# Depthwise convolution in eight phases: two channel tiles summed on VectorE, the other taps in half pairs, the last exchange on another queue

## The chip, the cores and the metric

The program runs on one core of one Trainium2 chip. The metric is the device time of one execution in microseconds (us). Before the change it is 1882.76 us, the median of three runs (1879.57 to 1883.23). The core has five engines that run side by side, each in its own order: PE (TensorE, with PEld, its weight load), DVE (VectorE), ACT (ScalarE), POOL (GpSimd) and SP (SyncE, which here only issues transfers). 0.2% of the time is 3.8 us.

## What is computed

Two model blocks are computed for 512 tokens of width 1024. The change touches one layer of the second block, a convolution module; everything else stands.

```
def conformer_conv(x, w_pw1, b_pw1, w_dw, b_dw, ln_g, ln_b, w_pw2, b_pw2):
    a = jax.nn.glu(x @ w_pw1 + b_pw1, axis=-1)
    y = lax.conv_general_dilated(
        a, w_dw[:, None, :].astype(a.dtype), window_strides=(1,),
        padding=((CONV_WIDTH - 1, 0),),
        dimension_numbers=('NWC', 'WIO', 'NWC'),
        feature_group_count=D_MODEL) + b_dw
    y = jax.nn.silu(layernorm(y, ln_g, ln_b))
    return y @ w_pw2 + b_pw2
```

`x` is the RMS-normed stream, 512 tokens by 1024 channels. The middle step is causal and depthwise: each channel has 31 taps (`CONV_WIDTH`), and each output token is the sum of 31 earlier gated values of the same channel, each times its tap. The layer norm then takes mean and variance over all 1024 channels of a token, so no token can be normalised before all channels are summed.

## The kernel before

Tensors stand with channels on the 128 partitions, so 1024 channels are 8 tiles (`t` = 0 to 7) of 128 x 512. A dense product is done in three fp32r matmuls for each weight block (high x high, high x low, low x high; lines 395 to 397). Its weights come in units of 128 x 1024. For each unit SP loads `raw` (line 338, two buffers), ACT rounds it into `wH` (line 373) and DVE subtracts to get `wL` (line 374).

`ph_con` computes the convolution module. For each tile `t` PE runs a **dense block**, the 48 matmuls of units 2t and 2t+1, which give the two halves of the gated unit. After the next dense block is written out, `open_gates(t)` puts on DVE: two scalings out of PSUM (`cg`, `ca`), a memset, and the gated product `glu` (line 1476); on ACT the sigmoid between them; then two weight splits (`wH`, `wL`) for the dense block after next; and, by `to_phases`, an **exchange** on SP: the tile is written to DRAM (`ph`*t*`x`, line 1425) and read back in eight pieces (`xp`, line 1428), so that the partitions hold 8 phases of the time axis x 16 channels. In this layout the 31 taps of 16 channels are 5 matrices of 128 x 128, and PE does the depthwise sum (`taps`, line 1438). Tiles are taken two by two: a pair is 80 matrix products, which the hardware runs as 160 matmuls of 64 columns each. The matrices come from DRAM, packed by the host in blocks (`mat`) of 16, 1 MB each, five for a pair, twenty in all. POOL issues them (line 1411) in the order of use, into the eight buffers that the activations `x` (four of them) also use.

DVE then adds the bias out of PSUM (`take`, line 1448) into `Y` and takes the layer norm's statistics (line 1453). When the last pair is through, a short serial stretch makes mean and scale (lines 1521 to 1537), and the output product follows.

Each engine runs its instructions in the order in which the code is written. This is the order that the change touches:

```
                    open_gates(t - 1)
                    if t in (4, 6):
                        pair(t // 2 - 2)
                    if t in (5, 7):
                        taken(t // 2 - 2)
                open_gates(last)
...
                pair(2)
                W = [self.unit(ahead=0) for _ in range(4)]
                taps(3, halves[0])
                taken(2)
```

So PE runs pair 0 after dense block 4, pair 1 after dense block 6, pair 2 after dense block 7, and pair 3 last; the exchange of tile 7 is issued by SP after `open_gates(7)`.

Of the kernel before, what the change touches and what calls it, by code (L numbers as in the profile page):

```python
# [10 lines left out]
F32 = mybir.dt.float32  # L11
# [42 lines left out]

RP, GC, NQ = 8, 16, 64

NMAT = 5
# [172 lines left out]
def matrix_order():  # L230

    return [(2 * i + j, g, m) for i in range(NT // 2) for g in range(P // GC) for m in range(NMAT) for j in range(2)]

# [37 lines left out]
class Builder:  # L271
# [1116 lines left out]
    def ph_con(self, ph):  # L1388
        nc, tc = self.nc, self.tc
        x = self.x  # L1390
        with tc.tile_pool(name="pc", bufs=1) as pool:
# [9 lines left out]
            nc.sync.dma_start(out=both, in_=self.kst_d[:, KC["both"][0]:KC["both"][0] + P])  # L1401
            gates, glus, xs, banks, mats = {}, {}, {}, {}, []
            place = {key: n for n, key in enumerate(matrix_order())}
# [15 lines left out]
            def padded(name):  # L1419
                return pool.tile([P, W_], F32, tag="glu", name=self.nm(name), bufs=8)  # L1420


            def to_phases(t):
                d = self.dp.tile([P, W_], F32, name=f"ph{t}x")
                nc.sync.dma_start(out=d, in_=glus.pop(t))
                xp = xs[t] = padded("xp").rearrange("p (g q) -> p g q", g=P // GC)
                for s in range(RP):
                    nc.sync.dma_start(out=xp[GC * s:GC * s + GC],
                                      in_=bass.AP(d.tensor, d.offset + s * q_, [[W_, GC], [GC * W_, P // GC], [1, q_]]))
# [21 lines left out]
            def statistics(i, b):  # L1451
                for r in range(RP):
                    nc.vector.bn_stats(stat[:, r, 2 * i + b, :], Y[:, i, r, b * 64:b * 64 + 64])

            halves = [range(4), range(4, 8)]

            def pair(i):
                for gs in halves:
                    taps(i, gs)

            def taken(i):
                for b, gs in enumerate(halves):
                    take(i, gs)
                    statistics(i, b)

            def open_gates(u):
                pa, pg = gates.pop(u)
                a, g = self.tmp(name="ca"), self.tmp(name="cg")
                nc.vector.tensor_tensor(g, pg, rb, ALU.mult)
                nc.vector.tensor_tensor(a, pa, rb, ALU.mult)  # L1470
                nc.scalar.activation(g, g, AF.Sigmoid, bias=self.col("b_pw1", 8 + u))
                glu = glus[u] = padded("glu")
                view = lambda v: v.rearrange("p (q r) -> p r q", r=RP)
                o = glu.rearrange("p (r q) -> p r q", r=RP)
                nc.vector.memset(o[:, :, :NMAT - 1], 0.0)
                nc.vector.scalar_tensor_tensor(o[:, :, NMAT - 1:], view(a), self.col("b_pw1", u), view(g),
                                               ALU.add, ALU.mult)
                to_phases(u)
                for _ in range(2):
                    if self.u_split <= self.u_used + 2:  # L1480
                        self.split()

            last = NT - 1
            with tc.manual_schedule():
# [5 lines left out]
                for t in range(1, NT):  # L1490
# [6 lines left out]
                    gates[t] = pa, pg  # L1497
                    open_gates(t - 1)
                    if t in (4, 6):
                        pair(t // 2 - 2)  # L1500
                    if t in (5, 7):
                        taken(t // 2 - 2)
                open_gates(last)

                nc.scalar.activation(self.small([P, 1]), self.ones[:, 0:1], AF.Silu)
                pair(2)
                W = [self.unit(ahead=0) for _ in range(4)]
                taps(3, halves[0])
                taken(2)

# [292 lines left out]
```

## Time and profile before

| what | us |
|---|---|
| median of three runs | 1882.76 |
| the profiled execution | 1881.89 |
| its span, first to last instruction | 1880.1 |
| PE busy (9386 matmuls) | 1839.6 (98%) |
| DVE busy | 941.0 (50%) |
| ACT busy | 696.0 (37%) |
| POOL busy | 242.9 (13%) |

The span is the stretch that the trace covers; the profiled execution's own time is 1.8 us more. PE is busy nearly all the time, so a change elsewhere moves the time only where PE stands still or is given less to do. Two of the 40 slices of the page (47 us each) show PE below 9 tenths. One of them, from 893 to 940 us, holds the end of the convolution module. PEclk is the clock that the throttle granted to PE; it has two levels, 2.4 GHz (shown as 1.00) and 1.2 GHz (0.50). The convolution module runs from 766.9 to about 984 us of the span.

### The profile page before, as it was taken

To read this page: it belongs to the slowest core of one execution; us is meant where nothing else is said; L and a number is where in the kernel's file an instruction comes from. 1 tells how busy PE (TensorE), PEld (TensorE's weight loads), DVE (VectorE), ACT (ScalarE), POOL (GpSimd) and SP (SyncE) were. 2 spreads that over 40 slices of the span, in tenths; PEclk is the share of its full clock that TensorE was granted. 3 is DMA by queue.
4 is the path that set the end of the run, shared out by engine and by line. 5 is a ranking of instruction groups with operands and counts; after the bars stand their busy time and mean duration, and the time that the engine had idled before them with its cause. 6 is when DMAs were issued, how large, how long until landed. Compare 5 with 4: busy or idle time off the path is not lost.

```text
span 1880.1 us, 23726 instructions
## 1 busy us (share of the span) xinstructions
PE 1839.6 (98%) x9386; PEld 1508.0 (80%) x9386; DVE 941.0 (50%) x1667; ACT 696.0 (37%) x1145; POOL 242.9 (13%) x243
## 2 busy tenths in 40 slices
PE   9999999999999999999799999999999999999997
PEld 6877778888888888878578888888877888888886
DVE  6567755655343444444455434335677543343444
ACT  5546644444232324212243222123566432232232
POOL 0111011020000001101021101011254211010110
PEclk9999999999999999999899999999999999999998
DMA  5223222132323323577223332654211223222321
GB/s 195 96 68 124 90 90 79 57 96 90 101 91 100 101 90 101 174 232 284 77 90 108 103 101 91 108 158 136 90 59 45 79 90 101 92 96 93 101 90 55
DMA packets 68112, 198.57 MB, mean 106 GB/s; under 512 B 15344, under 2 KB 23152, under 8 KB 65440
## 3 DMA queue, kind: packets, MB, share of 16 engines
q1 hardware_dynamic: 61744, 169.96, 28.2%
q0 software_dynamic: 3584, 24.12, 4.4%
q10 hardware_dynamic: 2672, 2.97, 0.5%
q8 instruction: 74, 1.21, 0.3%
q14 instruction: 38, 0.31, 0.0%
HBM read 189.55 MB, written 7.47 MB: 105 GB/s over the span
## 4 chain that ended last, share of the span: by engine, by line
PE 81%; issue 8%; DVE 4%; DMA 3%; ACT 2%; POOL 1%; SPq 0%; POOLq 0%; ACTq 0%; DVEq 0%
PE mm L395 25%; PE mm L396 25%; PE mm L397 24%; DVE wL L374 1%; DMA mat<-in_mat_dram 1%; DMA raw<-in_w_dram 1%; PE pc L1438 1%; ACT wH L373 1%; PE bo L1756 1%; DVE q L1664 1%; PE fs L879 1%; PE ft L894 1%; PE fo L907 1%; DMA ph7x<-glu 0%; PE bs L1713 0%
## 5 line engine op out<-in xcount | busy, mean ns | idle before, releaser
L373 ACT CAST wH<-raw 128x1024 fp32r<-128x1024 f32 (+1 forms) x304 | 315.9, 1041 | 910.1 <-PE mm L396 615.3
L395 PE MATMUL mm<-xH,wH 128*128 128x512 f32 x1232 | 482.4, 392 | 0.0
L396 PE MATMUL mm<-xL,wH 128*128 128x512 f32 x1232 | 480.5, 390 | 0.7 <-DVE xL L536 0.7
L397 PE MATMUL mm<-xH,wL 128*128 128x512 f32 x1232 | 480.4, 390 | 0.0
L374 DVE TENSOR_TENSOR wL<-raw,wH 128x1024 fp32r<-128x1024 f32 (+1 forms) x304 | 371.5, 1223 | 144.2 <-ACT wH L373 137.1
L395 PEld LDWEIGHTS mm<-xH,wH 128*128 128x128 f32 x1232 | 231.8, 188 | 49.7 <-issue 2.2
L396 PEld LDWEIGHTS mm<-xL,wH 128*128 128x128 f32 x1232 | 231.7, 188 | 48.6 <-DVE xL L536 1.1
L397 PEld LDWEIGHTS mm<-xH,wL 128*128 128x128 f32 x1232 | 231.5, 188 | 48.2
L395 PE MATMUL mm<-hidH,wH 128*128 128x512 f32 (+1 forms) x615 | 238.2, 387 | 0.0
L396 PE MATMUL mm<-hidL,wH 128*128 128x512 f32 (+1 forms) x615 | 238.1, 387 | 0.0
L397 PE MATMUL mm<-hidH,wL 128*128 128x512 f32 (+1 forms) x615 | 238.0, 387 | 0.0
L549 DVE TENSOR_TENSOR h<-mm,h 128x512 f32<-128x512 f32 x103 | 71.1, 691 | 262.4 <-PE mm L397 262.4
L498 POOL TENSOR_TENSOR ssq<-ssq,sq 128x512 f32<-128x512 f32 (+1 forms) x49 | 77.8, 1587 | 627.1 <-ACT sq L497 620.4
L1371 POOL TENSOR_TENSOR g<-g,rbc 128x512 f32<-128x512 f32 x44 | 75.0, 1705 | 538.7 <-ACT g L1370 538.7
L395 PEld LDWEIGHTS mm<-hidH,wH 128*128 128x128 f32 x615 | 115.5, 188 | 24.0 <-issue 0.6
L396 PEld LDWEIGHTS mm<-hidL,wH 128*128 128x128 f32 x615 | 115.6, 188 | 23.5
L397 PEld LDWEIGHTS mm<-hidH,wL 128*128 128x128 f32 x615 | 115.5, 188 | 23.3
L1372 DVE TENSOR_TENSOR g<-mm,g 128x512 f32<-128x512 f32 x44 | 30.1, 690 | 124.1 <-PE mm L397 119.5
L1369 DVE TENSOR_TENSOR g<-mm,rbc 128x512 f32<-128x512 f32 x44 | 30.2, 691 | 99.2 <-PE mm L397 97.6
L1338 DVE SCALAR_TENSOR_TENSOR u<-mm,rbc 128x512 f32<-128x512 f32 x32 | 22.0, 691 | 77.0 <-PE mm L397 75.8
L395 PE MATMUL mm<-wH,xH 128*128 128x512 f32 (+1 forms) x160 | 60.3, 377 | 0.0
L397 PE MATMUL mm<-wH,xL 128*128 128x512 f32 (+1 forms) x160 | 59.0, 369 | 0.0
(326 smaller groups left out, 2296.3 us busy)
## 6 DMA issues: line engine op xcount, KB each, us to landing
raw<-in_w_dram SPq DMA_DIRECT2D x272, 512.0 KB, 3.5
mat<-in_mat_dram POOLq DMA_DIRECT2D x20, 1024.0 KB, 9.7
raw<-in_w_dram SPq DMA_DIRECT2D x32, 448.0 KB, 3.2
rel<-rt POOLq DMA_DIRECT2D x1, 3072.0 KB, 36.3
h<-in_x_dram SPq DMA_DIRECT2D x8, 256.0 KB, 5.1
raw<-in_w_dram SPq DMA_DIRECT2D x8, 256.0 KB, 5.3
bias<-rel SPq DMA_DIRECT2D x1, 2048.0 KB, 8.8
mem<-in_mem_dram ACTq DMA_DIRECT2D x4, 256.0 KB, 4.4
```

What stands on the lines that cost most here:

```text
L373: self.nc.scalar.copy(H[:, :n], raw[:, :n])
L374: self.low = lambda: self.nc.vector.tensor_tensor(L[:, :n], raw[:, :n], H[:, :n].bitcast(F32), ALU.subtract)
L395: mm(out, lhsT=aH, rhs=bH, start=start, stop=False)
L396: mm(out, lhsT=aH, rhs=bL, start=False, stop=False)
L397: mm(out, lhsT=aL, rhs=bH, start=False, stop=stop)
L498: (eng or nc.gpsimd).tensor_tensor(self.ssq[:, :n], self.ssq[:, :n], q[:, :n], ALU.add)
L549: nc.vector.tensor_tensor(self.h[:, t, :], ps, self.h[:, t, :], ALU.add)
L879: nc.tensor.matmul(ps[j][:, :n], lhsT=q[rs, t, bs], rhs=k[rs, t, :n], start=x == 0, stop=False)
L1338: nc.vector.scalar_tensor_tensor(t, ps, 0.0, rb, ALU.max, ALU.mult)
L1369: nc.vector.tensor_tensor(g, pg, rb, ALU.mult)
L1371: nc.gpsimd.tensor_tensor(g, g, rb, ALU.mult)
L1372: nc.vector.tensor_tensor(g, pu, g, ALU.mult)
```

## The change

Tiles 0 and 1 (`DIRECT`) are not exchanged and need no matrices. DVE sums their 31 taps itself: 31 instructions for each tile, each over 128 x 512 values, alternating between two accumulators, and one addition of the two (`chains`). `fill` places these instructions among the others of `open_gates`, by the numbers in `CHAIN`. PE then turns the two sums into the layout of `Y` by products with the identity (`turned`), and DVE adds the bias (`taken_direct`).

Tiles 2 to 7 stay with the matrices, which are now 15 blocks. Their taps stand in half pairs of 40 matrix products: pair 1 after dense blocks 5 and 6, the first half of pair 2 after dense block 7, then the rest of pair 2 and pair 3. The exchange of tile 7 is issued by POOL, and ahead of it are the issues of the first eleven matrix blocks; the last four follow it. The shared buffers of `glu` and `xp` are six, not eight.

```diff
-    return [(2 * i + j, g, m) for i in range(NT // 2) for g in range(P // GC) for m in range(NMAT) for j in range(2)]
+    return [(2 * i + j, g, m) for i in range(1, NT // 2) for g in range(P // GC) for m in range(NMAT) for j in range(2)]
...
+DIRECT, CHAIN = [0, 1], (6, 8, 8, 8, 10, 14, 14, 8)
...
             def to_phases(t):
+
+                eng = nc.gpsimd if t == NT - 1 else nc.sync
                 d = self.dp.tile([P, W_], F32, name=f"ph{t}x")
-                nc.sync.dma_start(out=d, in_=glus.pop(t))
+                eng.dma_start(out=d, in_=glus.pop(t))
...
+            def chains():
+                for t in DIRECT:
+                    while t not in glus:
+                        yield
+                    acc = [pool.tile([P, S], F32, tag="cy", name=self.nm("cy"), bufs=3) for _ in range(2)]
+                    for k in range(TAPS):
+                        a, tap = acc[k % 2], glus[t][:, 2 + k:2 + k + S]
+                        if k < 2:
+                            nc.vector.tensor_scalar(a, tap, wd(t, k), None, ALU.mult)
+                        else:
+                            nc.vector.scalar_tensor_tensor(a, tap, wd(t, k), a, ALU.mult, ALU.add)
+                        yield
+                    nc.vector.tensor_tensor(acc[0], acc[0], acc[1], ALU.add)
+                    done[t] = acc[0]
+                    yield
...
+            def turned():
+
+                for b in range(2):
+                    ps = banks["direct", b] = self.bank("pc")
+                    for r in range(4):
+                        for j in range(2):
+                            nc.tensor.matmul(ps[j * NQ:j * NQ + NQ, r * P:(r + 1) * P],
+                                             lhsT=done[j][:, 4 * b + r::RP], rhs=self.ident, start=True, stop=True)
+
+            def taken_direct():
+                for b in range(2):
+                    nc.vector.tensor_tensor(Y[:, 0, 4 * b:4 * b + 4, :],
+                                            banks.pop(("direct", b)).rearrange("p (r c) -> p r c", r=4),
+                                            bdw[:, 0, :].unsqueeze(1).to_broadcast([P, 4, P]), ALU.add)
+                for b in range(2):
+                    statistics(0, b)
...
-            def open_gates(u):
+            def open_gates(u, steps):
...
                 nc.scalar.activation(g, g, AF.Sigmoid, bias=self.col("b_pw1", 8 + u))
+                fill(2)
                 glu = glus[u] = padded("glu")
...
                 for _ in range(2):
                     if self.u_split <= self.u_used + 2:
-                        self.split()
+                        self.split_high()
+                        fill(2)
+                        self.split_low()
+                fill(steps - 6)
...
-                    open_gates(t - 1)
-                    if t in (4, 6):
-                        pair(t // 2 - 2)
-                    if t in (5, 7):
-                        taken(t // 2 - 2)
-                open_gates(last)
+                    if t == last:
+                        load_matrices(11 - len(mats))
+                    open_gates(t - 1, CHAIN[t - 1])
+
+                    if t >= 5:
+                        i, b = (t - 3) // 2, (t - 5) % 2
+                        taps(i, halves[b])
+                    if t >= 6:
+                        taken((t - 4) // 2, (t - 6) % 2)
+                open_gates(last, CHAIN[last])
...
-                pair(2)
+                for _ in chain:
+                    pass
+                taps(2, halves[1])
+                taken(2, 0)
+                turned()
                 W = [self.unit(ahead=0) for _ in range(4)]
+                taken(2, 1)
                 taps(3, halves[0])
-                taken(2)
+                taken_direct()
```

How this moves the instructions shows on two engines. First DVE, between `glu` of tile 5 and the scalings of tile 6. Here `wL` is a weight split, `cg` and `ca` are the scalings out of the PSUM banks `mm`, `cY` is a `take`, `cst` the statistics, and `cy` the two accumulators of the new chain. Before:

```order
L1476 SCALAR_TENSOR_TENSOR glu_7026<-ca_7021,cst,cg_7022 128x8x64
L374 TENSOR_TENSOR wL_7041<-raw_6945,wH_7040 128x1024
L374 TENSOR_TENSOR wL_7047<-raw_6951,wH_7046 128x1024
L1469 TENSOR_TENSOR cg_7195<-mm_6972,rbc_6490 128x512
L1470 TENSOR_TENSOR ca_7194<-mm_6971,rbc_6490 128x512
```

After the change, DVE's rows from the second weight split of this block on:

```order
L1477 SCALAR_TENSOR_TENSOR cy_6877<-glu_6591,cst,cy_6877 128x512
L1477 SCALAR_TENSOR_TENSOR cy_6878<-glu_6591,cst,cy_6878 128x512
L1477 SCALAR_TENSOR_TENSOR cy_6877<-glu_6591,cst,cy_6877 128x512
L1477 SCALAR_TENSOR_TENSOR cy_6878<-glu_6591,cst,cy_6878 128x512
L1477 SCALAR_TENSOR_TENSOR cy_6877<-glu_6591,cst,cy_6877 128x512
L1477 SCALAR_TENSOR_TENSOR cy_6878<-glu_6591,cst,cy_6878 128x512
L1477 SCALAR_TENSOR_TENSOR cy_6877<-glu_6591,cst,cy_6877 128x512
L1477 SCALAR_TENSOR_TENSOR cy_6878<-glu_6591,cst,cy_6878 128x512
L1453 TENSOR_TENSOR cY<-pc_6883,cb 128x8x64
L1458 BN_STATS cst_6353<-cY 128x6 x8
L1509 TENSOR_TENSOR cg_7138<-mm_6927,rbc_6490 128x512
L1510 TENSOR_TENSOR ca_7137<-mm_6926,rbc_6490 128x512
```

Eight rows of the chain of tile 1 and one `take` with its statistics now stand ahead of the scalings of tile 6; six more rows of the chain stand earlier in the block.

Second POOL, its issues from the matrices of pair 2 on. `mat` is a matrix block, `ph7x` the copy of tile 7 in DRAM, `xp` its eight pieces (`x8`). Before, the last seven issues:

```order
L1411 DMA mat_7320<-in_mat_dram 128x2048
L1411 DMA mat_7338<-in_mat_dram 128x2048
L1411 DMA mat_7363<-in_mat_dram 128x2048
L1411 DMA mat_7381<-in_mat_dram 128x2048
L1411 DMA mat_7399<-in_mat_dram 128x2048
L1411 DMA mat_7436<-in_mat_dram 128x2048
L1411 DMA mat_7454<-in_mat_dram 128x2048
```

After, the last ten:

```order
L1414 DMA mat_7129<-in_mat_dram 128x2048
L1414 DMA mat_7131<-in_mat_dram 128x2048
L1414 DMA mat_7133<-in_mat_dram 128x2048
L1414 DMA mat_7135<-in_mat_dram 128x2048
L1430 DMA ph7x<-glu_7237 128x544
L1433 DMA xp_7242<-ph7x 16x8x68 x8
L1414 DMA mat_7353<-in_mat_dram 128x2048
L1414 DMA mat_7371<-in_mat_dram 128x2048
L1414 DMA mat_7408<-in_mat_dram 128x2048
L1414 DMA mat_7426<-in_mat_dram 128x2048
```

The exchange of tile 7 has come from SP's queue into POOL's, behind the first block of pair 3 and ahead of the four others.

## Rows read from the trace of the kernel before

**Rows 1.** The chain that ended last: start us, us, what.

```profile
882.97 1.17 DVE glu L1476
884.16 8.96 DMA ph7x<-glu
...
896.40 6.26 DMA xp<-ph7x
```

**Rows 2.** Timeline of PE: start us, us, line, out<-in, count [idle before <-releaser].

```profile
821.38 0.39 PE L395 MATMUL mm<-xH,wH 128*128 128x512 f32 x1
822.06 0.39 PE L395 MATMUL mm<-xH,wH 128*128 128x512 f32 x1
822.83 7.21 PE L1438 MATMUL pc<-mat,xp 128*64 128x128 f32 x128
833.73 3.68 PE L1438 MATMUL pc<-mat,xp 128*64 128x128 f32 x32 [3.70 <-DMA mat<-in_mat_dram]
...
881.38 9.17 PE L1438 MATMUL pc<-mat,xp 128*64 128x128 f32 x162
902.80 11.10 PE L1438 MATMUL pc<-mat,xp 128*64 128x128 f32 x158 [12.25 <-DMA xp<-ph7x]
```

**Rows 3.** Stretches: us, busy and count of PE, PEld, DVE, ACT, POOL; PEclk, DMA share, GB/s.

```profile
832.00:834.00 2.00, 0.27 (x2) 0.27 (x4) 0.00 (x0) 0.37 (x1) 0.00 (x0) 0.54 1.06 440
...
881.30:902.80 21.50, 9.25 (x164) 8.96 (x163) 8.26 (x24) 4.19 (x5) 2.10 (x4) 0.79 0.96 361
...
888.00:892.00 4.00, 2.55 (x46) 2.31 (x42) 2.10 (x9) 1.04 (x1) 0.00 (x0) 1.00 1.01 419
```

**Rows 4.** Timeline of POOL: issues of transfers.

```profile
878.81 1.05 POOL L1411 DMA_DIRECT2D mat<-in_mat_dram  x2 [7.61 <-PE mm L397]
...
885.40 0.53 POOL L1411 DMA_DIRECT2D mat<-in_mat_dram  x1 [1.22 <-PE pc L1438]
```

**Rows 5.** Transfers by line, 760 to 930 us: count, KB each, median us to landing.

```profile
mat<-in_mat_dram POOLq DMA_DIRECT2D x20, 1024.0 KB, 9.7
...
ph5x<-glu SPq DMA_DIRECT2D x1, 272.0 KB, 2.1
xp<-ph5x SPq DMA_DIRECT2D x8, 34.0 KB, 1.9
...
ph7x<-glu SPq DMA_DIRECT2D x1, 272.0 KB, 9.0
```

**Rows 6.** Timeline of DVE, four places.

```profile
172.48 2.72 DVE L800 SCALAR_TENSOR_TENSOR fqL<-ps,s,fqH 128x512 fp32r<-128x512 f32 x4
...
862.77 2.42 DVE L374 TENSOR_TENSOR wL<-raw,wH 128x1024 fp32r<-128x1024 f32 x2
865.11 0.68 DVE L1448 TENSOR_TENSOR cY<-pc,cb 128x512 f32<-128x512 f32 x1
865.83 1.12 DVE L1453 BATCH_NORM_STATS2 cst<-cY 128x6 f32<-128x64 f32 x8
...
881.49 0.69 DVE L1469 TENSOR_TENSOR cg<-mm,rbc 128x512 f32<-128x512 f32 x1 [9.25 <-PE mm L397]
882.10 0.68 DVE L1470 TENSOR_TENSOR ca<-mm,rbc 128x512 f32<-128x512 f32 x1
```

**Rows 7.** Groups of DVE, whole span: busy us, mean ns of one | idle before.

```profile
L551 DVE SCALAR_TENSOR_TENSOR h<-mm,cst,h 128x512 f32<-128x512 f32 x8 | 6.0, 750 | 9.5 <-PE mm L397 9.5
```

**Rows 8.** Timeline of POOL and of DVE where two instructions meet.

```profile
954.59 1.31 POOL L498 TENSOR_TENSOR ssq<-ssq,sq 128x512 f32<-128x512 f32 x1 [0.92 <-ACT sq L497]
954.67 1.78 DVE L536 SCALAR_TENSOR_TENSOR xL<-h,cst,xH 128x512 fp32r<-128x512 f32 x1
```

**Rows 9.** Line 1411 and tile xp, time to landing: least, median, longest.

```profile
DMA to landing us min/median/max: 5.2/9.7/16.0
...
DMA to landing us min/median/max: 1.8/2.1/11.7
```

**Rows 10.** Line 1428, the issues of one exchange's eight pieces: least, median, longest ns.

```profile
L1428 SPq DMA_DIRECT2D xp<-ph1x x8: 319/429/1812, 799.4 to 804.0; - x8
```

More of the change, by code (lines that the diff above doesn't have):

```diff
@@ L1401, in ph_con @@
             nc.sync.dma_start(out=both, in_=self.kst_d[:, KC["both"][0]:KC["both"][0] + P])
-            gates, glus, xs, banks, mats = {}, {}, {}, {}, []
+            wd = lambda t, k: self.col("w_dw", t * TAPS + k)
+            gates, glus, xs, banks, mats, done = {}, {}, {}, {}, [], {}
             place = {key: n for n, key in enumerate(matrix_order())}
@@ L1419, in padded @@
             def padded(name):
-                return pool.tile([P, W_], F32, tag="glu", name=self.nm(name), bufs=8)
+                return pool.tile([P, W_], F32, tag="glu", name=self.nm(name), bufs=6)
             def to_phases(t):
+                eng = nc.gpsimd if t == NT - 1 else nc.sync
                 d = self.dp.tile([P, W_], F32, name=f"ph{t}x")
-                nc.sync.dma_start(out=d, in_=glus.pop(t))
+                eng.dma_start(out=d, in_=glus.pop(t))
                 xp = xs[t] = padded("xp").rearrange("p (g q) -> p g q", g=P // GC)
                 for s in range(RP):
-                    nc.sync.dma_start(out=xp[GC * s:GC * s + GC],
+                    eng.dma_start(out=xp[GC * s:GC * s + GC],
                                       in_=bass.AP(d.tensor, d.offset + s * q_, [[W_, GC], [GC * W_, P // GC], [1, q_]]))
@@ L1455, in ph_con, with taken, fill @@
             halves = [range(4), range(4, 8)]
[L1457 to L1464, printed above, removed]
-            def open_gates(u):
+            def taken(i, b):
+                take(i, halves[b])
+                statistics(i, b)
+            def chains():
[13 more added lines that the diff above has]
+                    yield
+            chain = chains()
+            def fill(n):
+                for _ in range(n):
+                    next(chain, None)
+            def turned():
[13 more added lines that the diff above has]
+            def open_gates(u, steps):
                 pa, pg = gates.pop(u)
@@ L1471, in open_gates @@
                 nc.scalar.activation(g, g, AF.Sigmoid, bias=self.col("b_pw1", 8 + u))
+                fill(2)
                 glu = glus[u] = padded("glu")
[L1473 to L1478, printed above, removed]
+                if u in DIRECT:
+                    nc.vector.memset(glu[:, :W_ - S], 0.0)
+                    nc.vector.scalar_tensor_tensor(glu[:, W_ - S:], a, self.col("b_pw1", u), g, ALU.add, ALU.mult)
+                else:
+                    view = lambda v: v.rearrange("p (q r) -> p r q", r=RP)
+                    o = glu.rearrange("p (r q) -> p r q", r=RP)
+                    nc.vector.memset(o[:, :, :NMAT - 1], 0.0)
+                    nc.vector.scalar_tensor_tensor(o[:, :, NMAT - 1:], view(a), self.col("b_pw1", u), view(g),
+                                                   ALU.add, ALU.mult)
+                    to_phases(u)
                 for _ in range(2):
                     if self.u_split <= self.u_used + 2:
-                        self.split()
+                        self.split_high()
+                        fill(2)
+                        self.split_low()
+                fill(steps - 6)
             last = NT - 1
```

## The prediction

> **What bounds the kernel now.** I read the busy shares first: PE 98%, DVE 50%. A change that gives DVE more work can pay only where PE waits, or where PE gets less to do. Next I read the chain of waits that ended last. In the convolution module it leaves PE for its longest detour: glu of tile 7 starts at 882.97 and takes 1.17, its copy to DRAM is issued at 884.16 and takes 8.96, the last of its eight pieces goes out at 896.40 and takes 6.26 [rows 1]. PE's timeline shows the price: pair 2 runs at 881.38 for 9.17, then PE stands for 12.25, and pair 3 starts at 902.80 [rows 2]. Pair 0 is the second place: 128 matmuls, 3.70 of waiting for a matrix block, 32 more [rows 2]. The third is the clock: over pair 2 with the wait behind it the granted clock is 0.79 on average, and in the short wait it had fallen near the lower level, 1.2 GHz: 0.54 for 832 to 834 [rows 3]. Pair 3 shows what that costs: 11.10 for 160 matmuls that pair 2 does in 9.17 [rows 2].
>
> The exchange is slow because of what flies with it. POOL issues six matrix blocks of 1 MB between 878.81 and 885.40 [rows 4], and the DMA engines are busy 0.96 of that stretch [rows 3]. With next to nothing beside it, tile 5's copy lands in 2.1, its pieces in 1.9; tile 7's copy needs 9.0 [rows 5].
>
> **The change part by part.** I go by the span's clock and ask when the last tap of pair 3 ends: 902.80 + 11.10 = 913.9 before [rows 2]. What follows (statistics, scale, output product) is the same code, so I move it as a block.
>
> *PE, taken away and moved.* Within a product the matmuls of line 395 start 0.68 apart, every third one, so 0.227 each [rows 2], and a dense block of 48 takes 10.9. Taps at the full clock take 7.21/128 = 0.0563 each [rows 2], a half pair of 80 takes 4.5. Pair 0 and its wait leave PE: dense block 5 begins where pair 0 did, at 822.8. Three dense blocks and two half pairs later dense block 7 ends at 822.8 + 32.7 + 9.0 = 864.5; before it ended at 881.4, where pair 2 starts [rows 2]. That is 16.9 gained so far. I cost no matrix wait here: blocks 0 to 3 are loaded long before, as they were, and those that pairs 1 and 2 need are issued a dense block or more ahead, 10.9 against a median landing of 9.7 [rows 5]; the cover gone, one wait is 3.7 [rows 2].
>
> *DVE, added.* The chain has 64 instructions over 128 x 512. Four fp32 instructions of this kind take 2.72 in a row, 0.68 each [rows 6]; a single one 0.75 [rows 7]. I take 0.68, since neighbours in the chain use different accumulators and need not wait for each other; 0.79 (0.75 and a short gap) is the other end. The chain is 64 x 0.68 = 43.5 of new work on an engine that waits, in order, for PE, ACT and transfers.
>
> The block of one tile on DVE, without the chain, is two scalings at 0.61 from start to start [rows 6], the memset and glu 1.3 (the latter 1.17 [rows 1]), two weight splits 2.4 [rows 6]: 4.9. With ten rows of the chain (tile 4) it is 11.7, against 10.9 of PE. With fourteen rows and a take with its statistics, 0.68 + 1.12 [rows 6], it is 4.9 + 9.5 + 1.8 = 16.2 (tiles 5 and 6), against a dense block and a half pair, 15.4. So DVE falls back by 0.8 three times, 2.4, and I allow 0.6 for weights that land late: the scalings of tile 7 start 3.0 after dense block 7, not at once. What is queued behind them is glu 7 and the exchange. From dense end to the end of glu 7 it was 2.7 (881.4 to 884.1 [rows 1, 2]). Glu 7 ends at 864.5 + 3.0 + 2.7 = 870.2. Bounds: 867.2 with no lag, 878 with 0.79 for each row (below).
>
> The weight splits stand between rows of the chain, so PE could wait for weights. It does not at 0.68: the splits of tile u feed dense block u+2, which starts one dense block later at the earliest, and at most six rows, 4.1, stand ahead of the second split.
>
> At a place where DVE and POOL meet, a DVE instruction with two SBUF inputs, 0.75 elsewhere, took 1.78 while POOL ran one of 1.31 [rows 7, 8]. The Trainium skill (SBUF — State Buffer, "Who interferes with whom") says that a DVE instruction with two SBUF inputs shares its second read with GpSimd instructions that read SBUF, but not with ones that only write it; the two rows agree with the first half. In the convolution POOL only issues transfers; by that section the chain would run undisturbed, and were each of POOL's seven issues of about 0.53 in the chain's time to hold up one row, glu 7 would end up to 3.7 later.
>
> *The exchange, moved to POOL's queue.* SP no longer waits in it, so SP's next weight loads come earlier; they had time. On POOL it waits behind block 10, whose buffer comes free 2.6 before dense block 7 ends (878.81 against 881.4 [rows 2, 4]), so at 862: before glu 7. Blocks 9 and 10 land by about 869, so the copy has little beside it. I take: issue 0.5, landing 2.1 [rows 5] plus 0.4 for POOL's slower start, eight issues at POOL's 0.53 each [rows 4] 4.2, the last piece 1.9 + 0.4 [rows 5]. Sum 9.5 against 18.6 before (884.1 to 902.7 [rows 1]). POOL's start is bounded below by 0 and above by 2.7, the least landing of a matrix block, 5.2 [rows 9], less the 2.5 that 1 MB takes at 419 GB/s [rows 3]. The pieces are in at 870.2 + 9.5 = 879.7.
>
> *The end.* PE does pair 2 from 864.5 to 873.5 and the 16 turning products, 32 matmuls at tap rate, to 875.3 (twice that would still lie in the wait). It then stands for 4.4 and loses the clock, as it did in 3.70 [rows 2, 3]. Pair 3 at the rate of the cold start before, 11.1 [rows 2], would end at 890.9. But four of its five blocks are issued only behind the eight pieces, from about 877.4. The first lands after 5.2 at the least, 9.7 at the median [rows 9]; the median was taken among rival transfers, so I take 7.0: 884.4. The others follow at 2.5 (1 MB at the 419 GB/s of 888 to 892; 361 in the mixed stretch gives 2.9 [rows 3]): 891.9. Sixteen products at the mixed rate, 11.1/5 = 2.2, end at 894.1. So matrices, not PE, end last.
>
> Sum: 913.9 - 894.1 = 19.8 less. The profiled execution took 1881.89, so 1862.1; the median lies 0.87 above that execution, so **1863**.
>
> **The rivals.** *DVE is the bound.* If each chain row takes 0.79, tile blocks of eight rows (4.9 + 6.3 = 11.2) already exceed 10.9. Tiles 4 to 6 carry 38 rows: 38 x 0.11 = 4.2, the earlier ones add about 1, and each lag delays an exchange, thus SP's weight loads behind it, for which DVE then waits: about 3 more. Glu 7 ends at 878.4, the pieces are in at 887.9, the last block at 900.1, the end at 902.3: 11.6 less, 1871. For it: DVE would be over 100% busy from 833 on. Against it: the row of four at 0.68.
>
> *The exchange stays slow.* If it still takes 18.6 because it shares engines with weight loads and with the blocks queued behind it, the pieces are in at 888.8; the four blocks, issued from about 886, land until 900.5, the end is 902.7: 11.2 less, 1872. The Trainium skill (DMA: Bandwidth & Descriptors, "Issuing engines are not separate DMA queues") speaks for this: transfers of all queues run on the same 16 engines, so another issuing engine saves only issue time. By it the queue alone gives nothing here; rows 5 show, too, that it is the company that counts, and that is moved as well.
>
> *Slower.* POOL's software queue could be bad at small pieces, for which the trace has no row on POOL. The nearest are SP's worst: 9.0 for the copy [rows 5], 1.81 for an issue [rows 10], 11.7 for a piece [rows 9]. 870.2 + 0.5 + 9.0 + 8 x 1.81 + 11.7 = 905.9, and 11.1 of cold taps end at 917.0: 3.1 more than before, and with the late matrix blocks behind it (2.5 each for two of them still to come) up to 922: 1891. It decides from pieces that land at 902.8, an exchange of 32.6.
>
> *It ends early.* No lag, exchange 9.1, first block after 5.2: 867.2 + 9.1 = 876.3, last block at 874 + 5.2 + 7.5 = 886.7, end at 888.9 or below: 25 less, 1858.
>
> **How the numbers follow.** The forecast, 1860 to 1868: 0.52. Early, 1855 to 1860: 0.13. DVE bound and slow exchange, 1868 to 1876: 0.15 and 0.11. Within 0.2% (3.8 us, about what a measurement of this kernel can tell from no change; both losses together would do it): 0.04. Slower: 0.05. The range 1856 to 1875 leaves about 0.2 out. Faster 0.91, same 0.04, slower 0.05.
>
> **What would show it.** In the trace of after: dense block 7 ends near 864.5 and PE has no wait of over 1 us before it (wrong if weight splits or matrices hold it); chain rows start 0.68 apart; glu 7 ends near 870; copy to last piece takes 9 to 10, not 18; PE waits 4 to 5 for tile 7 and then for matrix blocks; the last tap ends near 894, and from there to the output product takes as long as before. A last tap later than 903, or a tail longer by some us because the clock stays at the lower level, would make the prediction wrong.

## The result, and the profile after the change

The changed kernel takes 1864.92 us, the median of four runs (1864.46 to 1865.66), against 1882.99 for the kernel before (1879.57 to 1885.10). The ratio is 0.9906, with a 95% interval of 0.9889 to 0.9923: 18.1 us less. The forecast was 1863, with a range of 1856 to 1875.

The page after shows the same busy share for PE, with a shorter span and fewer matmuls:

```profile
span 1863.0 us, 23506 instructions
...
PE 1830.1 (98%) x9258; PEld 1497.3 (80%) x9258; DVE 978.7 (53%) x1731; ACT 697.5 (37%) x1145; POOL 245.8 (13%) x247
```

Lines have moved: matrix blocks are issued by line 1414, taps are line 1443, the scalings 1509 and 1510, glu 1521, a take 1453, the chain 1477. The chain of waits that ended last (start us, us, what), which answers to [rows 1]:

```profile
855.96 8.85 DMA ph6x<-glu
864.86 5.91 DMA xp<-ph6x
870.78 3.96 DMA ph7x<-glu
...
875.02 3.33 POOL xp L1433 x7
...
878.73 2.15 DMA xp<-ph7x
880.88 14.14 DMA mat<-in_mat_dram
895.07 1.97 PE pc L1443 x32
```

The copy of tile 7 takes 3.96 where it took 8.96. The exchanges still end the stretch, but after tile 7's pieces the chain now goes through a matrix block that lands 14.14 after its issue. The timeline of PE (start us, us, line, out<-in, count, idle before and releaser) shows the same, and answers to [rows 2]:

```profile
849.91 4.59 PE L1443 MATMUL pc<-mat,xp 128*64 128x128 f32 x80
865.53 8.95 PE L1443 MATMUL pc<-mat,xp 128*64 128x128 f32 x160
874.32 2.11 PE L1495 MATMUL pc<-kst,cy 128*64 128x128 f32 x32
876.26 0.38 PE L1443 MATMUL pc<-mat,xp 128*64 128x128 f32 x2
883.11 5.27 PE L1443 MATMUL pc<-mat,xp 128*64 128x128 f32 x62 [6.47 <-DMA xp<-ph7x]
890.00 1.97 PE L1443 MATMUL pc<-mat,xp 128*64 128x128 f32 x32 [1.62 <-DMA mat<-in_mat_dram]
892.59 1.97 PE L1443 MATMUL pc<-mat,xp 128*64 128x128 f32 x32 [0.62 <-DMA mat<-in_mat_dram]
895.07 1.97 PE L1443 MATMUL pc<-mat,xp 128*64 128x128 f32 x32 [0.51 <-DMA mat<-in_mat_dram]
```

Half pairs of 80, as at 849.91, stand between dense blocks with no wait, dense block 7 ends at 865.5, and PE waits 6.47 for tile 7 where it waited 12.25. Then it waits three times for a block, 2.75 in all. The last tap ends at 897.04 instead of 913.9. From there to the end of the span both kernels take 966.0 to 966.2, so the whole difference lies in this stretch.

The timeline of DVE, in pieces:

```profile
842.92 5.39 DVE L1477 SCALAR_TENSOR_TENSOR cy<-glu,cst,cy 128x512 f32<-128x512 f32 x8
...
850.02 0.69 DVE L1509 TENSOR_TENSOR cg<-mm,rbc 128x512 f32<-128x512 f32 x1
...
851.23 1.41 DVE L1477 SCALAR_TENSOR_TENSOR cy<-glu,cst,cy 128x512 f32<-128x512 f32 x2
854.57 0.09 DVE L1520 MEMSET glu<- 128x32 f32 x1 [1.94 <-PE pc L1443]
...
867.86 0.68 DVE L1509 TENSOR_TENSOR cg<-mm,rbc 128x512 f32<-128x512 f32 x1
...
869.33 1.16 DVE L1521 SCALAR_TENSOR_TENSOR glu<-ca,cst,cg 128x512 f32<-128x512 f32 x1 [0.15 <-ACT cg L1511]
...
877.62 1.23 DVE L376 TENSOR_TENSOR wL<-raw,wH 128x1024 fp32r<-128x1024 f32 x1 [5.39 <-ACT wH L375]
```

Eight chain rows take 5.39, 0.67 each. The scalings of tile 7 start 2.3 after dense block 7, glu 7 ends at 870.5. Up to tile 6 DVE keeps pace: its scalings start at 850.02, 0.1 behind dense block 6 (PE's half pair at 849.91). There is one new wait, 1.94 for a buffer (six are shared by `glu` and `xp`), and after glu 7 and one `take` DVE stands idle for 5.39. Last, POOL and SP:

```profile
862.95 1.05 POOL L1414 DMA_DIRECT2D mat<-in_mat_dram  x2 [7.59 <-PE mm L399]
870.78 0.56 POOL L1430 DMA_DIRECT2D ph7x<-glu  x1 [6.77 <-DVE glu L1521]
875.02 4.24 POOL L1433 DMA_DIRECT2D xp<-ph7x  x8 [3.69 <-DMA ph7x<-glu]
879.25 2.16 POOL L1414 DMA_DIRECT2D mat<-in_mat_dram  x4
...
872.50 8.44 SPq L340 DMA_DIRECT2D raw<-in_w_dram  x4
```

POOL issues the copy, the pieces and the last four blocks one behind the other. The copy goes out 0.3 after glu 7, with all blocks ahead of it too (below), so on POOL it is glu 7 that it waits for, and not the pieces of tile 6 that stand before it in the chain above. Beside these transfers, from 872.50 to 880.94, SP issues four weight units of the output product, 512 KB each.

### The profile page after: what moved, and what is told of

It reads as the page before. It is cut to its first block, busy times and chain, and to the rows that moved or that the text cites. A ratio compares the mean times of both kernels' runs of the same rounds, so it can differ in the third digit from the quotient of the medians.

```text
span 1863.0 us, 23506 instructions
## 1 busy us (share of the span) xinstructions
PE 1830.1 (98%) x9258; PEld 1497.3 (80%) x9258; DVE 978.7 (53%) x1731; ACT 697.5 (37%) x1145; POOL 245.8 (13%) x247
## 4 chain that ended last, share of the span: by engine, by line
PE 84%; DVE 5%; issue 4%; DMA 3%; ACT 2%; POOL 1%; SPq 0%; POOLq 0%; ACTq 0%; DVEq 0%
PE mm L397 26%; PE mm L398 26%; PE mm L399 26%; DVE wL L376 1%; DMA raw<-in_w_dram 1%; DVE cy L1477 1%; DMA mat<-in_mat_dram 1%; PE bo L1813 1%; DVE q L1721 1%; PE fs L881 1%; PE ft L896 1%; PE fo L909 1%; ACT wH L375 1%; PE ps L507 0%; DMA ph6x<-glu 0%
## 5 line engine op out<-in xcount | busy, mean ns | idle before, releaser
L376 DVE TENSOR_TENSOR wL<-raw,wH 128x1024 fp32r<-128x1024 f32 (+1 forms) x304 | 371.4, 1222 | 121.1 <-ACT wH L375 114.0
```

The lines of the kernel that those rows point to most:

```text
L376: self.low = lambda: self.nc.vector.tensor_tensor(L[:, :n], raw[:, :n], H[:, :n].bitcast(F32), ALU.subtract)
```

## Experiments

The runs of one kernel scatter by 1 to 7 us, which is as much as some of the differences. So beside each median stands the **stretch**, read from the trace: from the start of tile 0's first scaling (785.45 before, 786.03 after) to the end of the last tap. Median less stretch is 1752 to 1756, so the two agree in the large. The stretch is of one execution, which need not be the median one: among others it was the fastest of its kernel for the chain left out, for both together and for two blocks fewer, and the slowest, by 2.7, for the weights behind blocks alone.

| kernel | median us | stretch us |
|---|---|---|
| before | 1882.99 | 128.4 |
| after | 1864.92 | 111.0 |
| before, pair 0 left out | 1869.57 | 115.2 |
| before, exchange moved | 1879.53 | 125.1 |
| after, whole pairs | 1867.49 | 114.0 |
| after, exchange on SP | 1871.71 | 118.6 |
| after, all blocks ahead | 1872.03 | 119.5 |
| after, two blocks ahead | 1865.72 | 112.0 |
| after, chain left out | 1865.12 | 109.3 |
| after, chain behind glu 7 | 1864.52 | 109.9 |
| after, weights behind blocks | 1863.95 | 111.7 |
| chain behind glu 7, pieces on two queues | 1864.85 | 110.5 |
| the same, and weights behind blocks | 1862.25 | 107.2 |
| chain behind glu 7, two blocks fewer | 1862.89 | 107.4 |

The kernel before ran beside each group again, at 1881.54 to 1881.88 over 7 to 13 runs, 1.1 to 1.4 below the 1882.99. The changed kernel was not run again, so that a difference of 1 or 2 us from its 1864.92 shows nothing.

My theory going in: most of the gain is the time of pair 0 on PE; the exchange gains by the company that it flies in, not by its queue; DVE is not the bound; what is left is the four blocks behind the exchange. The rivals: PE's time alone explains all; POOL's queue itself is faster; DVE is the bound.

### How the gain divides: three parts, each alone

**Pair 0 off PE**, in the kernel before, with nothing on DVE for it:

```diff
...
-                    if t in (4, 6):
-                        pair(t // 2 - 2)
...
+                    if t == 6:
+                        pair(1)
...
+                    if t == 5:
+                        nc.vector.tensor_copy(Y[:, 0], bdw[:, 0].unsqueeze(1).to_broadcast([P, RP, P]))
```

> The kernel before, with pair 0 left out: no taps and no matrices for tiles 0 and 1, whose sum is replaced by the bias (this part of the computation is missing); no work on VectorE in its place, whole pairs, the exchange of tile 7 on SP among the matrices as before. Theory (PE's time leaves the path in full, so nearly all of the change's 17 to 18 us is this): 7.21 + 3.68 + 3.70 of wait = 14.6 to 15.3 less, 1867 to 1869 us, dense block 7 ends near 866, the exchange still takes about 18. Rival (the exchange and the matrices set the end, so that PE's removal moves only the wait): gain below 8, 1875 or more.

Measured: 1869.57 (1867.97 to 1872.28), 12.2 less than the 1881.73 beside it, where the theory had 14.6 to 15.3; the stretch is 13.2 shorter. PE's timeline:

```profile
853.92 3.56 PE L1438 MATMUL pc<-mat,xp 128*64 128x128 f32 x32 [2.15 <-DMA mat<-in_mat_dram]
868.52 9.17 PE L1438 MATMUL pc<-mat,xp 128*64 128x128 f32 x162
888.87 11.79 PE L1438 MATMUL pc<-mat,xp 128*64 128x128 f32 x158 [11.19 <-DMA xp<-ph7x]
```

Of the 14.6 that pair 0 took with its wait, 1.1 come back as a longer wait in pair 1 (2.15, before 1.06). The wait for tile 7 is nearly what it was, 11.19. So the time left the path almost whole, and the rival falls. The run also loads five blocks fewer, as the changed kernel does; what PE's work and what these loads are worth was not taken apart.

**The exchange moved**, in the kernel before:

```diff
+                eng = nc.gpsimd if t == NT - 1 else nc.sync
...
-                nc.sync.dma_start(out=d, in_=glus.pop(t))
+                eng.dma_start(out=d, in_=glus.pop(t))
...
+                    if t == last:
+                        load_matrices(16 - len(mats))
```

> The kernel before with one part of the change alone: the exchange of tile 7 on POOL, behind the first 16 matrix blocks and ahead of the last four. Theory (company, not queue: the four blocks no longer fly with the exchange, but they are late by as much): the exchange takes 12 to 15 instead of 18.6, PE starts pair 3 at about 898, waits for blocks that land until about 908, and the last tap ends at 909 to 911: 3 to 5 less than before, about 1878 to 1880 us. Rival (it is worth what after gained beyond pair 0's time, 5 or more): 1877 or less. Second rival (holding back four blocks costs what the exchange gains): no change, 1882.

Measured: 1879.53 (ratio to before 0.9987, 0.9978 to 0.9997), 2.0 less; the stretch is 3.4 shorter. PE:

```profile
896.35 6.29 PE L1439 MATMUL pc<-mat,xp 128*64 128x128 f32 x62 [6.71 <-DMA xp<-ph7x]
903.02 1.97 PE L1439 MATMUL pc<-mat,xp 128*64 128x128 f32 x32 [0.38 <-DMA mat<-in_mat_dram]
...
908.46 1.97 PE L1439 MATMUL pc<-mat,xp 128*64 128x128 f32 x32 [0.50 <-DMA mat<-in_mat_dram]
```

The wait for tile 7 falls from 12.25 to 6.71, and part of that is given back to blocks that come late.

**Half pairs undone**, in the changed kernel:

```diff
-                    if t >= 5:
-                        i, b = (t - 3) // 2, (t - 5) % 2
-                        taps(i, halves[b])
-                    if t >= 6:
-                        taken((t - 4) // 2, (t - 6) % 2)
+                    if t == 6:
+                        taps(1, halves[0])
+                        taps(1, halves[1])
+                    if t == 7:
+                        taken(1, 0)
+                        taken(1, 1)
...
+                taps(2, halves[0])
                 taps(2, halves[1])
```

> The changed kernel with its half pairs undone: pair 1 in one piece after dense block 6, pair 2 in one piece after dense block 7. Theory (the halves save the wait for a block inside pair 1: 2.2 in the run with pair 0 left out, where pair 1 is whole): dense block 7 ends 2 to 2.5 later, and with it all that follows: 1866 to 1868 us. Rival (the blocks of pair 1 are loaded long before here, as VectorE has taken pair 0's place: no wait): 1864 to 1866. Second rival (DVE gets both takes late and lags more): 1868 or more.

Measured: 1867.49, 2.6 more; the stretch is 3.0 longer. My number held, but only half of its reason. PE waits 1.39 for a block inside pair 1; the other part is DVE, as the second rival has it: both takes now stand ahead of tile 7's scalings:

```profile
867.11 0.68 DVE L1453 TENSOR_TENSOR cY<-pc,cb 128x512 f32<-128x512 f32 x1
...
868.86 0.67 DVE L1453 TENSOR_TENSOR cY<-pc,cb 128x512 f32<-128x512 f32 x1
...
870.59 0.67 DVE L1509 TENSOR_TENSOR cg<-mm,rbc 128x512 f32<-128x512 f32 x1
```

The scalings start at 870.59, 2.7 later than in after; dense block 7 ends 1.0 later. The three parts alone make 12.2 + 2.0 + 2.6 = 16.8, against 16.6 to 18.1 in one, by the runs of the kernel before that one takes. That this fits is chance, as the next runs show: with its exchange on SP the changed kernel takes 1871.71, 2.1 more than the kernel before with pair 0 left out, and the exchange's new place is then worth 7, not 2.0.

### Queue or company

**The exchange on SP again** (`eng = nc.sync`), so that the last four blocks no longer wait behind it:

> The changed kernel, with the exchange of tile 7 issued by SP again, as before the change. POOL no longer waits for it, so the last four matrix blocks go out as their buffers come free, from about 865.5 on, and fly with the exchange. Theory (what counts is the company, and the new queue matters because it holds the matrices back): the copy takes about 9 and the pieces 6, as tile 6's do in the trace of after (8.9, 6.8); the pieces are in at about 887 instead of 883, the matrices wait for nobody, pair 3 runs its 11.1 of cold taps and ends near 898, against 897.0: 1864 to 1868 us. Rival (the exchange's place gives several us by itself): the time goes up by 6 or more, to 1871, since the old exchange took 18.6. Second rival (PE's removed work is all, the exchange's place nothing): 1864 to 1866.

**All blocks ahead of it, on POOL:**

```diff
+                load_matrices(15 - len(mats))
                 open_gates(last, CHAIN[last])
```

> The changed kernel, exchange of tile 7 on POOL, but all four last matrix blocks are issued ahead of it (their buffers are free at about 865.5 to 869, glu 7 ends at 870.5). The company is that of the run with the exchange on SP, only the queue differs. Theory (company, not queue): within 2 us of that run, the last piece in at 885 to 889. Rival (POOL's queue is itself what is faster): copy 4, pieces 2.6 each as in after, last piece in by 881 to 883, the matrices early, last tap at 883 + 11.1 = 894, 3 us less than after: 1862.

Measured: 1871.71 and 1872.03, 7 us more than after. Two queues, one company, the same time, as my theory had it for the second run; so what the exchange gains is that four blocks stand behind it. For the first run my number was wrong (1864 to 1868), and the rival's was right: 1871, the exchange's place is worth 6 or more. The two runs come to their time in different ways. The chain of waits of the run on SP:

```profile
863.36 13.79 DMA xp<-ph6x
...
877.21 9.63 DMA ph7x<-glu
```

Among the blocks the pieces of tile 6 take 7.6 to 19.0; the line shows the third, 13.79. On SP the copy of tile 7, ready at 869.2, goes out only at 877.21, when that third piece has landed, takes 9.63, and PE starts pair 3 at 892.39. The trace tells what holds it: SP's transfers report their landing through eight semaphores (counters that an engine can wait for), taken in turn, and none of the 377 that have eight ahead of them on SP goes out before the one eight places ahead has landed. The two weight loads between pieces and copy go out at 870.20 and 873.15, behind the landing of the first and second piece (870.13, 873.09), the copy behind that of the third (877.14). On POOL the copy goes out at 870.52, takes 15.0, and PE starts at 893.80. PE's timeline with all blocks ahead:

```profile
886.18 0.66 PE L1443 MATMUL pc<-mat,xp 128*64 128x128 f32 x2 [9.99 <-DMA xp<-ph6x]
893.80 11.46 PE L1443 MATMUL pc<-mat,xp 128*64 128x128 f32 x158 [6.97 <-DMA xp<-ph7x]
```

I had not reckoned with tile 6: its pieces, too, now come late.

**Two of the four blocks ahead** (`load_matrices(13 - len(mats))` at the same place):

> The changed kernel with two of the four last matrix blocks (11 and 12) issued ahead of the exchange, two behind it. Theory (after is held by four blocks that come 2.5 apart behind the exchange, the last at 895): two blocks are in by about 874, the exchange is at most 1.5 later (884.5), the last two blocks land at about 890 to 891, pair 3 ends at 884.5 + 11.1 = 895.6 or so without waiting for a block; 1.5 us less, 1862 to 1864. Rival (the engines are full, so whatever goes ahead delays the exchange by as much): exchange 5 later (888), end 899, 1867.

Measured: 1865.72, no difference that can be told. PE has no wait for a block left, but tile 7 comes 3.8 later than in after (886.94), and the last tap ends at 897.3:

```profile
886.94 10.38 PE L1443 MATMUL pc<-mat,xp 128*64 128x128 f32 x158 [6.31 <-DMA xp<-ph7x]
```

The rival was right in kind, though its time (1867) was not reached: what goes ahead delays the exchange by what it saves. So with eleven or thirteen blocks ahead the time is the same; with all fifteen it is 7 us more.

### DVE, and what comes after it

**The chain left out** (`for k in range(3)` in place of all 31 taps) and **its last eight rows behind glu 7** (`CHAIN` ends in `14, 6, 6`, and no rows ahead of glu 7 itself):

> The changed kernel with only 3 of the 31 taps of tiles 0 and 1 summed on VectorE (28 of 31 chain rows of each tile are left out, so those two tiles' sums are not the convolution's). Theory (the chain's price on the path is the lag with which tile 7's scalings start after dense block 7, 2.4 in after, and nothing else): glu 7 ends at about 868, exchange, matrices and the last tap each 2 to 2.5 earlier, 1862 to 1863 us. Rival (DVE is the bound through the stretch, each row counts): 56 rows x 0.68 = 38 of work gone and over 5 us gained, below 1860. Second rival (the transfers are the bound, so an earlier glu 7 only meets more company): within 1 us of 1865.

> The changed kernel with the last eight rows of tile 1's chain moved behind glu 7, into a stretch where DVE stands idle for 5.4 in after. Theory (the lag of 2.4 is all that the chain costs): the scalings of tile 7 start at dense block 7's end, glu 7 ends 2 to 2.4 earlier, and so does everything to the last tap: 1862 to 1863 us, the same as with the chain left out. Rival (the transfers are the bound): glu 7 is earlier, the copy slower by as much, 1865.

Measured: 1865.12 (1863.17 to 1866.77) and 1864.52: within 1 us of after, as the rival about the transfers said. In the traces the stretch is 1.7 and 1.1 shorter. DVE is not the bound: without 56 chain rows no gain can be told. PE with the rows behind glu 7:

```profile
879.52 3.46 PE L1443 MATMUL pc<-mat,xp 128*64 128x128 f32 x30 [3.15 <-DMA xp<-ph7x]
883.87 1.97 PE L1443 MATMUL pc<-mat,xp 128*64 128x128 f32 x32 [0.89 <-DMA mat<-in_mat_dram]
...
891.24 1.97 PE L1443 MATMUL pc<-mat,xp 128*64 128x128 f32 x32 [1.70 <-DMA mat<-in_mat_dram]
893.70 1.97 PE L1443 MATMUL pc<-mat,xp 128*64 128x128 f32 x32 [0.49 <-DMA mat<-in_mat_dram]
```

Glu 7 is 2.5 earlier and pair 3 starts 3.6 earlier, but the waits for blocks grow from 2.75 to 4.82. The blocks end the stretch.

### What holds the blocks

**Pieces on two queues:** ACT issues every second piece, on top of the run before.

```diff
-                    eng.dma_start(out=xp[GC * s:GC * s + GC],
+                    (nc.scalar if t == NT - 1 and s % 2 else eng).dma_start(out=xp[GC * s:GC * s + GC],
```

> The changed kernel with the last eight chain rows behind glu 7 (as in the run that tried this alone, 1864.5, last tap at 895.7) and, besides, every second of tile 7's eight pieces issued by ACT instead of POOL. Theory (from the copy's landing on the transfers are the bound, and they stand partly idle, 153 to 198 GB/s, while POOL issues eight pieces at 0.53 each): the pieces are out in 2.1 instead of 4.2, the last four blocks go out 2.1 earlier, the last tap ends at 893.5 to 894: 1862 to 1863 us. Rival (the earlier blocks slow the pieces by as much): 1864 to 1865.

Measured: 1864.85, nothing gained: the rival held. The issues take 2.1 less and the blocks go out at 875.2, but copy and pieces land after 5.3 in the median, where they took 2.9.

**Two weight units behind the blocks**, in the changed kernel: SP's loads of 878.9 and 880.6 are issued by POOL after the last block.

```diff
...
+                self.hold = True
                 taps(2, halves[1])
...
                 taps(3, [7])
+                self.behind = True
+                for _ in range(2):
+                    self.load()
+                self.behind = self.hold = False
```

> The changed kernel with two weight units (0.5 MB each) that SP loads at 878.6 and 880.5, beside the pieces of tile 7 and the last matrix blocks, issued by POOL behind the last block instead. Theory (the last four blocks are late because they share the engines with these loads: 1 MB at 419 GB/s is 2.5): the last block lands 2 to 2.5 earlier, at about 892.7, PE's waits for blocks shrink from 2.8 to below 1, the last tap ends near 895: 1862 to 1863 us. Rival (the blocks are slow for themselves, or the exchange holds them): no change, 1864.5 to 1865.5.

Measured: 1863.95 (1863.62 to 1866.82): no gain that can be told. The trace is of the slowest of the four. POOL's timeline:

```profile
871.95 0.55 POOL L1432 DMA_DIRECT2D ph7x<-glu  x1 [6.77 <-DVE glu L1523]
878.86 4.23 POOL L1435 DMA_DIRECT2D xp<-ph7x  x8 [6.36 <-DMA ph7x<-glu]
883.08 2.15 POOL L1416 DMA_DIRECT2D mat<-in_mat_dram  x4
```

The last block is in at 896.9, 11.7 after the issue of the last four ends at 885.2, where after has 895.03 and 13.6 (881.41). But the copy takes 6.6 instead of 3.96. The two weight units ahead of those moved left SP at 868.2 here, not at 872.5, since the first piece of tile 6 landed at 865.9, not at 872.4. That they slow the copy was not tested, but the runs with eleven blocks ahead fit it: where the two units left at 868, the copy landed 5.2 (whole pairs) and 5.5 (here) after block 10, where they left at 871 to 873, in after and four others, 2.2 to 2.5; with the chain left out (865) 3.2.

**Both together:**

> The run before this one in the list, with the two weight units issued behind the last block as well. Theory (the transfers are the bound: 1 MB less beside the last blocks is 2.5): last tap at 891 to 892, 1860 to 1861 us. Rival (as in the run that moved these two alone, the two units ahead of them go out earlier, at 868, and meet the copy of tile 7, which took 6.6 there instead of 4.0): 1863 to 1865.

Measured: 1862.25 (1861.07 to 1863.54); ratio to before 0.9899 (0.9883 to 0.9915). It is the fastest here. Its four runs all lie below after's four, but the ratios to before overlap, so the times alone do not show that it beats after; they do for the run with pieces on two queues, which ran beside it. Here the first two weight units kept their place behind tile 6's pieces (872.07), and only the two beside the blocks were gone:

```profile
880.56 6.79 PE L1445 MATMUL pc<-mat,xp 128*64 128x128 f32 x94 [4.08 <-DMA xp<-ph7x]
888.72 1.97 PE L1445 MATMUL pc<-mat,xp 128*64 128x128 f32 x32 [1.36 <-DMA mat<-in_mat_dram]
891.08 1.97 PE L1445 MATMUL pc<-mat,xp 128*64 128x128 f32 x32 [0.39 <-DMA mat<-in_mat_dram]
```

Against the run with pieces on two queues, the only difference is that 1 MB of weights: 2.6 us in the median, 3.3 in the stretch (0.5 of it is clock that PE lost there, as the last section shows). It hardly goes out later: SP issued the two units at 878.7 and 880.6 there, POOL issues them at 879.3 and 881.0 here, and dense block 7, too, ends 0.7 later in this trace. On SP's queue they landed among the blocks (886.6 and 891.7, the last block at 893.2); on POOL's, behind the blocks, they land after them (892.3 and 893.5, the last block at 891.0). So what counts here is the queue that they stand in.

**Two blocks fewer:** the last 32 products use blocks 11 and 12 again, 2 MB less.

> The run with the last eight chain rows behind glu 7, with the last two matrix blocks not loaded: their 32 products use blocks 11 and 12 a second time (so the last groups of channels of tiles 6 and 7 get the wrong taps; PE's work is the same). Theory (the transfers, not PE, end the convolution): PE starts pair 3 at 879.5 as there, waits for a block by less than 1 instead of 4.8, and the last tap ends at 879.5 + 10.6 to 11.1 = 890 to 891 instead of 895.7: 1859 to 1860 us. Rival (PE's cold clock and the exchange are what is left): 1863 to 1864.5.

Measured: 1862.89 (1861.35 to 1865.68), last tap at 893.7, not 890 to 891. Less than half of the gain came, 1.6 in the median and 2.0 at the last tap (895.7), and the time lies just below the rival's 1863 to 1864.5:

```profile
884.49 1.97 PE L1444 MATMUL pc<-mat,xp 128*64 128x128 f32 x32 [0.42 <-DMA mat<-in_mat_dram]
888.20 5.46 PE L1444 MATMUL pc<-mat,xp 128*64 128x128 f32 x96 [1.74 <-DMA mat<-in_mat_dram]
```

Blocks 11 and 12 still land at 884.5 and 888.2, as they did with two more queued behind them (883.9 and 887.6). So the blocks behind do not slow the ones ahead; the weight units, which fly beside them from another queue, do, by the run before this one.

## Why the prediction was right

The forecast was 19.8 less for the last tap; it ended 16.9 earlier, or 17.4 by the stretch. After's clock stands 0.6 later at the module's start; the forecasts below are as given.

| step | forecast | measured |
|---|---|---|
| dense block 7 ends | 864.5 | 865.5 |
| a chain row, start to start | 0.68 | 0.67 |
| lag of tile 7's scalings | 3.0 | 2.3 |
| glu 7 ends | 870.2 | 870.5 |
| exchange, from there until PE starts | 9.5 | 12.6 |
| last four blocks issued from | 877.4 | 879.25 |
| last block in | 891.9 | 895.03 |
| last tap ends | 894.1 | 897.04 |

**PE's part** was right: the 16.9 for dense block 7 came out as 881.4 - 865.5 = 15.9, or 16.5 with the clock's 0.6. Pair 0 left out gives 881.4 - 868.5 = 12.9 of it, the bulk. From 786 to 876 the profile shows no wait of PE, as forecast.

**DVE's part** was right in size, and the rival that DVE is the bound falls: rows 0.67 apart, and no gain from leaving the chain out. That the lag came near 3.0 is partly luck: I had DVE fall back by 0.8 with each of tiles 4 to 6, so by 1.6 at tile 6's scalings, and it lay back 0.1 there; of the 2.3 in the end 1.94 are a wait for one of six buffers, which I had not looked for. On the ports of SBUF: the chain's mean row took 752 ns against the 750 of [rows 7], and two rows that POOL's issue at 851.31 meets took 1.41, as two do elsewhere. This is what the Trainium skill (SBUF — State Buffer, "Who interferes with whom") lets one expect of a POOL that only issues transfers.

**The exchange** is the term that was too small, 9.5 against 12.6. The copy took 3.96 where I had 2.5, and the last piece 4.1, where I had 2.3. The step that failed is the sentence "Blocks 9 and 10 land by about 869, so the copy has little beside it", with the other that SP's weight loads "had time". Block 9 landed at 868.56, but block 10 at 872.23, and the pieces of tile 6, which I had left out, at 872.44 to 873.95; the copy landed at 874.74. The weight units, from 872.50 on, met only its end. What each of these cost the copy no run takes apart. The last piece went out at 878.73, just ahead of SP's third weight unit (878.88). With that unit and the fourth behind the blocks, no piece took longer than 2.2 (issue to landing of copy and pieces: least, median, longest; after, then weights behind blocks, where the 6.6 is the copy):

```profile
DMA to landing us min/median/max: 2.1/2.6/4.1
...
DMA to landing us min/median/max: 2.0/2.1/6.6
```

So for the pieces the weight units are what I had not counted. These rows also leave little of the 0.4 that I had put down for POOL's slower start: 2.0 to 2.2 on POOL against 1.9 for tile 5's pieces on SP [rows 5].

The rule of the Trainium skill (DMA: Bandwidth & Descriptors, "Issuing engines are not separate DMA queues") was borne out by the two runs with the same company on SP and on POOL, 1871.71 and 1872.03. By it the last two weight units, issued at nearly the same time, should cost the same from either queue; behind the blocks on POOL's they cost 2.6 us less than on SP's, and the measurement decides. The rival that rested on it needed the old company as well, and that had changed. The slower rival, POOL bad at small pieces, falls: pieces issue in 0.53 and the copy and pieces land after 2.1 to 4.1.

**The end** went as forecast in kind: PE waits, loses the clock (granted 0.50 from 882 to 886), starts, and then matrix blocks end last, some 2.5 apart (890.00, 892.59, 895.07). The last block landed 3.1 late. Of this 1.9 is the start of the four issues, at 879.25: the copy's 1.5 and glu 7's 0.3. The other 1.3 is the landing: the last block came 15.8 after 879.25, where I had 14.5. With two weight units behind the blocks it came 13.8 after the first of the four issues, so this part, too, goes to the weight units. The slow pieces move only PE's start; PE then waits for blocks in any case.

## What to carry to other kernels

When a change moves a short transfer out of a crowd, list everything that will be in flight then, the loads of the next stage among them, and ask which of it could go later; here 1 MB of weights that nobody needed yet cost 2.6 us in the run with pieces on two queues (in the changed kernel itself no gain could be told). To come later it need hardly be issued later: here it was enough to put it on the queue of the urgent transfers, behind them. Once a stretch is bound by transfers, an earlier producer (glu 7 by 2.5) or a faster issue gains little, since what it frees is met again as waits for the next transfer. A second engine with idle time can take over whole units of work from the engine that is the bound, as long as its rows can be placed so that they lag by less than the slack of what waits for them.

## What the runs showed of the hardware

A copy of 272 KB took 2.1 with little beside it [rows 5], 4.0 in after, 6.1 in the kernel before with its exchange moved, 9.6 and 15.0 where the last blocks were not held behind it: the time of a small transfer here goes with what flies with it and stands ahead of it. An issue on SP can also be held by an earlier transfer with which it shares no data: with the exchange on SP the copy of tile 7 went out at 877.21, just as the third piece of tile 6 had landed (877.14), whose semaphore it takes over. So small pieces that land late hold back what SP issues after them.

Among the long transfers the queue does matter: blocks queued behind others on POOL did not slow those ahead (884.5 and 888.2 without them, 883.9 and 887.6 with them), while two weight units of 512 KB landed among the blocks from SP's queue and behind them from POOL's, which was worth 2.6 us. The Trainium skill (DMA: Bandwidth & Descriptors, "Queues, rings and completion order") says that each DMA engine takes its queues in turn and works through each in order, and these runs agree with that.

A short wait behind a cold start can cost the clock again. With the pieces on two queues PE waited 2.92 for a block after starting at the low clock, and the stretch behind that wait (us; busy and count of PE, PEld, DVE, ACT, POOL; granted clock, DMA share, GB/s) reads

```profile
890.00:894.00 4.00, 3.70 (x38) 3.70 (x40) 0.00 (x0) 0.00 (x0) 0.00 (x0) 0.59 0.25 104
```

0.59, so near 1.2 GHz again, while after, which waited 1.62, 0.62 and 0.51 there, has 1.00 from 890 on. The last 64 matmuls took 5.38 there, where twice 32 take 3.94 at the full clock. As the last block landed only at 893.17, the end came 0.5 later for it (895.68 against 893.17 + 1.97).
